# A third couple by seven products of sums in every gate and up group of a decoder trunk

## The chip, the cores and the metric

The kernel runs on one core of a Trainium2 chip. The metric is the device time of one execution in microseconds (us), the median of several runs. TensorE multiplies matrices (PE in the profile, its weight loads PEld), VectorE (DVE) and ScalarE (ACT) do elementwise work, GpSimd (POOL) and SyncE (SP) mostly issue DMA transfers here.

## The reference, cut to what matters

The program is a two-layer decoder trunk on 256 tokens of width 2048: a Conformer convolution, a SwiGLU feed-forward block, shared keys and values, a dilated attention, a second SwiGLU block and a last RMSNorm, all in float32. The part that is touched is the first half of each SwiGLU block:

```
def _swiglu(h, w_gate, w_up, w_down):
    return (jax.nn.silu(h @ w_gate) * (h @ w_up)) @ w_down
```

`h` is 256 x 2048, `w_gate` and `w_up` are 2048 x 5632 and `w_down` is 5632 x 2048. There are two such blocks.

## The kernel before, in words

**Three passes.** A float32 product is made of three passes in a rounded type (fp32r): every operand is split into a high part and a remainder, and TensorE adds x_hi·w_hi, x_hi·w_lo and x_lo·w_hi into one bank (`nat`, L404 to L406). The split of a block of weights (`split`) is one cast on ACT (L216, it makes `whi`) and one subtraction on DVE (L218, it makes `wlo`). `whi` and `wlo` have four buffers each, and blocks are split two ahead of the block that TensorE works on (`AHEAD`).

**Groups and couples.** `ffn_hidden` makes the hidden layer in 11 groups of 512 gate columns and the same 512 up columns. A group sums over 2048 = 16 tiles of 128, taken as eight couples of two tiles. A couple done plainly ("n" in `ITEMS_FF`) is two blocks of 128 x 1024 weights, gate and up, and 2 (gate, up) x 2 (tiles) x 2 (token halves) x 3 passes = 24 matmuls of 512 columns. A couple marked "S" is done by Winograd's form of Strassen's scheme: the two tiles, the two token halves, gate and up make a 2 x 2 product of blocks, which takes seven products in place of eight, so 21 matmuls, some of them with sums of the activations (`xsums`) and some with sums of the weights. The items of a group are `"nnnnSnSn"` in every group but the first, which is all "n".

**The weights of an S couple.** `emit_sums` splits an S couple in four blocks q = 0 to 3. Block 0 is a split of a whole 128 x 1024 block, followed on DVE by four differences of 128 x 512 (L234: t1, t2, t4 and one more, written into the small buffers `sq` and `sqacc`). Blocks 1 to 3 are five splits of 128 x 512 each: one of raw weights, four of these differences. The raw weights of an S couple have one place only (`places`, three parts of the tile `work`). They are fetched by three DMAs on POOL's queue (`load_sums`, L205 for 512 KB, L207 twice for 256 KB), and the fetch for the next S couple can start only when the differences and splits of this one have read their part. The plain blocks come over SP's queue (L279) into three buffers `raw`.

**The end of a group.** After the last S couple `combine` brings the four sum banks to `work` (one ACT copy L875, four DVE additions L877). `hidden` adds them to the other four banks, applies SiLU on ACT (L884) and multiplies on DVE (L883, L886, L887). `turned`, five ticks into the next group, transposes the result on TensorE (L895), and ACT and DVE split it into `hid` (L897, L898). A tick is a step of the program's own queue (`later`), one for each block that TensorE has used. The sum banks of one group are the plain banks of the group before, so the first S couple has to come after `turned`.

**The activations' sums.** `sum_up` makes the four sums of a couple's activations once for each layer, during the first, all-plain group: one addition (L753), four small operations (L757), a cast on ACT (L758) and a remainder on DVE (L759).

Of the kernel before, what the change touches and what calls it, by code (L numbers as in the profile page):

```python
# [9 lines left out]
F32 = mybir.dt.float32  # L10
# [6 lines left out]
P = 128  # L17
# [23 lines left out]
SUMS = 7  # L41
# [2 lines left out]
ITEMS_1 = HALF_0, "nnn" + "SnnSnSn" * 2 + "Sn" + "nnn"  # L44


SUMS_FF = 2
ITEMS_FF = "nnnnSnSn"


_VEC = {}
# [39 lines left out]
def trunk(ctx: ExitStack, tc: tile.TileContext, xT, vec, const, w1, w2, wk, wv, wq, wo, wg0, wu0, wd0, wg1, wu1, wd1, fing, out):  # L91
# [211 lines left out]
    def later(n, fn):  # L303
        queue.append([n, fn])
# [441 lines left out]
    def wide(a):  # L746
        return a.rearrange("p (a b) -> p a b", b=P)

    def sum_up(sums, u, two, h, d):

        h, d = h.rearrange("p (a b) -> p a b", b=S), wide(d)
        two = two.bitcast(F32)
        nc.vector.tensor_tensor(out=h, in0=two[:, :, 0, :], in1=two[:, :, 1, :], op=ALU.add)  # L753
        a11, a21, a12, a22 = (h[:, j, t * P:(t + 1) * P] for j in range(2) for t in range(2))
        for i, a, b, op in ((0, a21, a22, ALU.add), (1, d[:, 0, :], a11, ALU.subtract), (2, a11, a21, ALU.subtract),
                            (3, a12, d[:, 1, :], ALU.subtract)):
            nc.vector.tensor_tensor(out=d[:, i, :], in0=a, in1=b, op=op)  # L757
        nc.scalar.copy(sums[:, u, :, 0, :], d)  # L758
        nc.vector.tensor_tensor(out=sums[:, u, :, 1, :], in0=d, in1=sums[:, u, :, 0, :].bitcast(F32), op=ALU.subtract)  # L759

    n_used = [0]

    def two_blocks(a, b, items, n_sums, n_rest, act, sums, cs, sum_banks, combine):


        u_sums, u_plain = pairs_of(items, n_sums)
        ab = a, b
        begun = [False, False]
        ps = None

        def plain(i, k, stop, ts=(0, 1), parts=None):
            hi, lo = parts or next_block(*ab[i], k)[1:]
            for j in range(GKV):
                for t in ts:
                    nat(cs[t][i], tokens(act, k * GKV + j, t), hi[:, j, :], lo[:, j, :], not begun[i] and j == 0, stop and j == GKV - 1)
            begun[i] = True

        def seven(k, start):
            n = n_used[0]
            n_used[0] += 1  # L780
            assert all_sums[n][0][0] is a[0] and all_sums[n][2] == k
            two = [[sums[:, k, i, j, :] for j in range(2)] for i in range(4)]
# [12 lines left out]
        for i in range(2):  # L795
            for k in ahead:
                plain(i, k, False)
                tick()
        body = items[2:len(items) - n_rest]
        for n, item in enumerate(body):  # L800
            if item == "S":
                if ps is None:
                    ps = [p for t in sum_banks() for p in t]
                    seven(next(u_sums), True)
                else:
                    seven(next(u_sums), False)
# [44 lines left out]
    def ffn_hidden(ff, scratch, wg, wu, x, norm):  # L851

        nonlocal hT
        hid = new_x(ff, "hid", FT)
        sums = ff.tile([P, SUMS_FF, 4, 2, P], F32R, name="xsums", tag="t8")
        later(2, lambda: norm.rstd_nat(bank2))
        for k in range(SUMS_FF):
            later(3 + 3 * k, lambda k=k: sum_up(sums, k, x[:, 2 * k:2 * k + 2, :, :], room("sq"), room("sq")))
        for n in range(2 * D // NBV):
            later(3 + n, lambda c=n // 2, t=n % 2: turn_over(c, t, bank2()[:, 0, :, :].rearrange("p a b -> p (a b)")))  # L860
            if n % 2:
# [60 lines left out]
    with tc.tile_pool(name="ff", bufs=1) as ff:  # L922
        scratch = kept.tile([P, DT * S], F32, name="residual")
        hid = ffn_hidden(ff, scratch, wg0, wu0, x, norm)
        buf = ff.tile([P, 4, NBV], F32, name="t", tag="t8")
        sums = rp.tile([P, SUMS, 4, 2, P], F32R, name="sums", tag="x")
        residual_back(8, scratch)
        later(6, lambda: load_first_sums(wd0, [buf[:, 0:2, :], buf[:, 2, :], buf[:, 3, :]]))
        for u in range(SUMS):
            later(2 + 3 * u, lambda u=u: sum_up(sums, u, hid[:, 2 * u:2 * u + 2, :, :], room("sq"), room("sq")))  # L930
# [12 lines left out]

        for half, items in enumerate(ITEMS_0):
            cs = (first_banks if half else second_banks)()
            rest, plain = two_blocks((wd0, 2 * half), (wd0, 2 * half + 1), items, items.count("S"), 3, hid, sums, cs,
                                     second_banks if half else first_banks, lambda ps: combine(half, ps))
            if half:
                x = new_x(rp, "x")
                norm = Norm()  # L950
                for c in range(2):
                    later(c, lambda c=c: normed(c))
            for i in range(2):
                for u in rest:
# [75 lines left out]
    with tc.tile_pool(name="ff", bufs=1) as ff:  # L1030
# [1 line left out]
        hid = ffn_hidden(ff, scratch, wg1, wu1, x, norm)  # L1032

        ss = [little("ss", 8) for t in range(2)]
        buf = ff.tile([P, 4, NBV], F32, name="t", tag="t8")
        gain = [buf[:, 2 + i, :] for i in range(2)]

        sums = rp.tile([P, SUMS, 4, 2, P], F32R, name="sums", tag="x")
        residual_back(8, scratch)
        later(6, lambda: table(AF.Sqrt, silu[-1]))  # L1040
        later(6, lambda: load_first_sums(wd1, [cst.rearrange("p (k n) -> p k n", k=GKV), buf[:, 0, :], buf[:, 1, :]]))
        for u in range(SUMS):
            later(2 + 3 * u, lambda u=u: sum_up(sums, u, hid[:, 2 * u:2 * u + 2, :, :], *gain))

        def load_gain(half):
            for i in range(2):
# [105 lines left out]
```

## Time and profile before

| | us |
|---|---|
| median of 3 runs (lowest, highest) | 2147.03 (2146.43, 2154.44) |
| profiled execution | 2150.78 |
| its span, first to last instruction | 2148.3 |
| busy in it: PE / DVE / ACT / POOL | 2124.0 / 1659.1 / 1157.6 / 342.4 |
| the 11 gate and up groups of the first layer | about 345 to 776 |
| the 11 of the second layer | about 1447 to 1878 |

Matmuls are pipelined: one of 512 columns is listed with 0.39 us, but the next starts 0.23 us after it. Likewise DVE and ACT start their next instruction a little before the listed end of the one before. Times on a row of the timeline count from the start of the span.

### The profile page before, as it was taken

To read this page: it belongs to the slowest core of one execution; us is meant where nothing else is said; L and a number is where in the kernel's file an instruction comes from. 1 tells how busy PE (TensorE), PEld (TensorE's weight loads), DVE (VectorE), ACT (ScalarE), POOL (GpSimd) and SP (SyncE) were. 2 spreads that over 40 slices of the span, in tenths; PEclk is the share of its full clock that TensorE was granted. 3 is DMA by queue.
4 is the path that set the end of the run, shared out by engine and by line. 5 is a ranking of instruction groups with operands and counts; after the bars stand their busy time and mean duration, and the time that the engine had idled before them with its cause. 6 is when DMAs were issued, how large, how long until landed. Compare 5 with 4: busy or idle time off the path is not lost.

```text
span 2148.3 us, 28961 instructions
## 1 busy us (share of the span) xinstructions
PE 2124.0 (99%) x10550; PEld 1801.0 (84%) x10550; DVE 1659.1 (77%) x2403; ACT 1157.6 (54%) x1611; POOL 342.4 (16%) x357
## 2 busy tenths in 40 slices
PE   8999899999999999999999999999999999999998
PEld 8999788888888887888888888888888888887886
DVE  6888875788888888878745677665887888788877
ACT  6665545455555555455644566554555555555454
POOL 4999111000000001001000100010000000011210
PEclk9999999999999999999999999999999999999999
DMA  7555367656665556655665644566666566666654
GB/s 244 183 159 168 97 182 233 194 196 193 199 198 194 189 193 225 206 187 184 194 197 184 190 150 148 174 198 213 199 188 214 179 198 200 200 205 222 211 203 155
DMA packets 115966, 410.66 MB, mean 191 GB/s; under 512 B 13936, under 2 KB 14960, under 8 KB 115824
## 3 DMA queue, kind: packets, MB, share of 16 engines
q1 hardware_dynamic: 93024, 331.19, 47.9%
q0 software_dynamic: 22080, 76.56, 10.9%
q8 instruction: 82, 1.34, 0.2%
q10 hardware_dynamic: 720, 1.07, 0.1%
q14 instruction: 60, 0.49, 0.1%
HBM read 402.47 MB, written 6.29 MB: 190 GB/s over the span
## 4 chain that ended last, share of the span: by engine, by line
PE 90%; DVE 4%; DMA 3%; ACT 1%; issue 1%; SPq 0%; POOL 0%; DVEq 0%; ACTq 0%; POOLq 0%
PE pp L405 10%; PE pp L406 10%; PE pp L404 10%; PE pp L331 10%; PE aux L404 8%; PE aux L406 8%; PE aux L405 8%; PE pp L373 7%; PE pp L335 5%; PE b L406 2%; PE b L404 2%; PE b L405 2%; DMA raw<-wd 2%; DVE wlo L218 2%; DVE aux L571 1%
## 5 line engine op out<-in xcount | busy, mean ns | idle before, releaser
L218 DVE TENSOR_TENSOR wlo<-raw,whi 128x1024 fp32r<-128x1024 f32 x400 | 483.3, 1231 | 189.6 <-ACT whi L216 188.2
L216 ACT CAST whi<-raw 128x1024 fp32r<-128x1024 f32 x400 | 412.7, 1051 | 351.9 <-DMA raw<-wu 93.0
L285 ACT CAST whi<-raw 128x1024 fp32r<-128x1024 f32 (+1 forms) x209 | 216.1, 1037 | 226.1 <-PE pp L331 84.2
L287 DVE TENSOR_TENSOR wlo<-raw,whi 128x1024 fp32r<-128x1024 f32 (+1 forms) x164 | 202.1, 1243 | 140.0 <-ACT whi L285 120.8
L404 PE MATMUL pp<-whi,x 128*128 128x512 f32 x668 | 261.2, 391 | 0.0
L406 PE MATMUL pp<-whi,x 128*128 128x512 f32 x668 | 260.1, 389 | 0.0
L405 PE MATMUL pp<-wlo,x 128*128 128x512 f32 x668 | 259.9, 389 | 0.0
L216 ACT CAST whi<-sq 128x512 fp32r<-128x512 f32 x128 | 79.6, 622 | 231.2 <-issue 83.1
L404 PE MATMUL aux<-whi,x 128*128 128x512 f32 x516 | 203.4, 394 | 0.0
L406 PE MATMUL aux<-whi,x 128*128 128x512 f32 x516 | 201.1, 390 | 0.0
L405 PE MATMUL aux<-wlo,x 128*128 128x512 f32 x516 | 200.9, 389 | 0.0
L406 PEld LDWEIGHTS pp<-whi,x 128*128 128x128 f32 x668 | 125.4, 188 | 26.1
L405 PEld LDWEIGHTS pp<-wlo,x 128*128 128x128 f32 x668 | 125.4, 188 | 25.7
L404 PEld LDWEIGHTS pp<-whi,x 128*128 128x128 f32 x668 | 125.4, 188 | 25.6
L571 DVE SCALAR_TENSOR_TENSOR aux<-up,vecs,aux 128x256 f32<-128x256 f32 x350 | 140.9, 481 | 1.6 <-ACT aux L569 1.6
L205 POOL DMA_DIRECT2D work<-wg x40 | 21.8, 546 | 747.4 <-DVE sqacc L234 565.5
L373 PE MATMUL pp<-x,whi 128*128 128x256 f32 x720 | 133.5, 287 | 0.0
L218 DVE TENSOR_TENSOR wlo<-sq,whi 128x512 fp32r<-128x512 f32 x128 | 88.3, 690 | 57.5 <-ACT whi L216 57.3
L331 PE MATMUL pp<-x,whi 128*128 128x512 f32 x512 | 122.7, 393 | 0.0
L405 PE MATMUL pp<-wlo,hid 128*128 128x512 f32 x306 | 119.8, 392 | 1.4 <-DVE wlo L218 1.1
L406 PE MATMUL pp<-whi,hid 128*128 128x512 f32 x306 | 119.2, 389 | 0.0
L404 PE MATMUL pp<-whi,hid 128*128 128x512 f32 x306 | 119.1, 390 | 0.0
(285 smaller groups left out, 4494.1 us busy)
## 6 DMA issues: line engine op xcount, KB each, us to landing
raw<-wg SPq DMA_DIRECT2D x136, 512.0 KB, 4.1
raw<-wu SPq DMA_DIRECT2D x136, 512.0 KB, 4.2
raw<-wd SPq DMA_DIRECT2D x128, 512.0 KB, 4.4
raw<-w SPq DMA_DIRECT2D x75, 512.0 KB, 3.9
work<-wg POOLq DMA_DIRECT2D x40, 512.0 KB, 3.8
work<-wu POOLq DMA_DIRECT2D x80, 256.0 KB, 4.2
raw<-wv SPq DMA_DIRECT2D x32, 512.0 KB, 4.3
raw<-wk SPq DMA_DIRECT2D x32, 512.0 KB, 4.2
```

The lines of the kernel that those rows point to most:

```text
L205: nc.gpsimd.dma_start(places[0], src[0])
L216: made.append(nc.scalar.copy(hi, raw))
L218: made.append(nc.vector.tensor_tensor(out=lo, in0=raw, in1=hi.bitcast(F32), op=ALU.subtract))
L285: nc.scalar.copy(hi[:, part, :], raw[:, part, :])
L287: eng.tensor_tensor(out=lo[:, part, :], in0=raw[:, part, :], in1=hi[:, part, :].bitcast(F32), op=ALU.subtract)
L331: nc.tensor.matmul(bk[:, m, :, :], hi, x[:, k, :, :], start=k == 0, stop=k == kt_n - 1 and turned, skip_group_check=True)
L335: nc.tensor.matmul(bk[:, m, 0, :], lo, x[:, k, 0, :], start=False, stop=k == kt_n - 1 and not turned, skip_group_check=True)
L373: nc.tensor.matmul(bks[u][:, m, :], a[:, j, m * P:(m + 1) * P], b, start=kt == 0 and m == 0 and i == 0, stop=kt == DT - 1 and i == len(pas ...
L404: nc.tensor.matmul(o, xs[0], hi, start=start, stop=False, skip_group_check=True)
L405: nc.tensor.matmul(o, xs[0], lo, start=False, stop=False, skip_group_check=True)
L406: nc.tensor.matmul(o, xs[1], hi, start=False, stop=stop, skip_group_check=True)
L571: nc.vector.scalar_tensor_tensor(out=acc[i % 2], in0=win, scalar=w, in1=acc[i % 2], op0=ALU.mult, op1=ALU.add)
```

## The change

Three couples of each group after the first are done by seven products, not two: the items are now `"nnnSnSSn"`, so the second and the third S couple follow each other with nothing between them. The sums of a third couple's activations need room. Three of the four sums of each couple stay in `xsums`; the fourth goes into the place of the couple's own first tile, second token half, in `x`, which an S couple does not read. So `sum_up` can write it only after the first group has used that couple, and its ticks move from 3 + 3k to 7 + 3k. It now casts and takes the remainder in two pieces (three sums, one sum). The tile `buf` of the later stages is made as large as the new `xsums`, with which it shares its room.

```diff
-SUMS_FF = 2
-ITEMS_FF = "nnnnSnSn"
+SUMS_FF = 3
+ITEMS_FF = "nnnSnSSn"
...
-        nc.scalar.copy(sums[:, u, :, 0, :], d)
-        nc.vector.tensor_tensor(out=sums[:, u, :, 1, :], in0=d, in1=sums[:, u, :, 0, :].bitcast(F32), op=ALU.subtract)
+        i = 0
+        for o in places:
+            di = d[:, i:i + o.shape[1], :]
+            nc.scalar.copy(o[:, :, 0, :], di)
+            nc.vector.tensor_tensor(out=o[:, :, 1, :], in0=di, in1=o[:, :, 0, :].bitcast(F32), op=ALU.subtract)
+            i += o.shape[1]
...
-        sums = ff.tile([P, SUMS_FF, 4, 2, P], F32R, name="xsums", tag="t8")
+        three = ff.tile([P, SUMS_FF, 3, 2, P], F32R, name="xsums", tag="t8")
+        sums = [(three[:, k, :, :, :], x[:, 2 * k:2 * k + 1, :, P:]) for k in range(SUMS_FF)]
...
-            later(3 + 3 * k, lambda k=k: sum_up(sums, k, x[:, 2 * k:2 * k + 2, :, :], room("sq"), room("sq")))
+            later(7 + 3 * k, lambda k=k: sum_up(sums[k], x[:, 2 * k:2 * k + 2, :, :], room("sq"), room("sq")))
```

What this does to the queues is seen at two places. The first is DVE's order at the end of the second S couple of a group (`wlo<-sq`, `wlo<-sqacc` are the splits of its last differences, `wlo<-raw` the split of a plain block). Before:

```order
L218 TENSOR_TENSOR wlo_4450<-sq_4413,whi_4449 128x512
L218 TENSOR_TENSOR wlo_4450<-sqacc_4415,whi_4449 128x512
L218 TENSOR_TENSOR wlo_4462<-sq_4419,whi_4461 128x512
L218 TENSOR_TENSOR wlo_4462<-sqacc_4417,whi_4461 128x512
L218 TENSOR_TENSOR wlo_4475<-raw_4473,whi_4474 128x1024
L218 TENSOR_TENSOR wlo_4487<-raw_4485,whi_4486 128x1024
```

and now:

```order
L218 TENSOR_TENSOR wlo_4457<-sqacc_4412,whi_4456 128x512
L218 TENSOR_TENSOR wlo_4469<-work_3786,whi_4468 128x1024
L234 TENSOR_TENSOR sq_4472<-work_3786 128x512
L234 TENSOR_TENSOR sqacc_4474<-work_3786,sq_4472 128x512
L234 TENSOR_TENSOR sqacc_4476<-work_3786,sqacc_4474 128x512
L234 TENSOR_TENSOR sq_4478<-work_3786 128x512
L218 TENSOR_TENSOR wlo_4487<-work_3786,whi_4486 128x512
L218 TENSOR_TENSOR wlo_4497<-sq_4472,whi_4496 128x512
L218 TENSOR_TENSOR wlo_4497<-sqacc_4474,whi_4496 128x512
L218 TENSOR_TENSOR wlo_4509<-sq_4478,whi_4508 128x512
L218 TENSOR_TENSOR wlo_4509<-sqacc_4476,whi_4508 128x512
L218 TENSOR_TENSOR wlo_4522<-raw_4520,whi_4521 128x1024
```

Where the plain blocks followed, the ten instructions of a third S couple now stand, and the plain blocks come after them. The second place is TensorE's order behind the first block of that last S couple. Before, its second block and the start of its third stood with their passes in turn:

```order
L404 MATMUL aux_4197<-whi_4433,xsums_3466 128x512
L405 MATMUL aux_4197<-wlo_4434,xsums_3466 128x512
L406 MATMUL aux_4197<-whi_4433,xsums_3466 128x512
L404 MATMUL pp_4360<-whi_4449,xsums_3466 128x512
L405 MATMUL pp_4360<-wlo_4450,xsums_3466 128x512
```

and now:

```order
L404 MATMUL aux_4228<-whi_4486,x_2831 128x512
L404 MATMUL pp_4355<-whi_4496,xsums_3466 128x512
L404 MATMUL pp_4354<-whi_4496,xsums_3466 128x512
L405 MATMUL aux_4228<-wlo_4487,x_2831 128x512
L406 MATMUL aux_4228<-whi_4486,x_2831 128x512
L404 MATMUL aux_4227<-whi_4508,x_2831 128x512
L405 MATMUL pp_4355<-wlo_4497,xsums_3466 128x512
L406 MATMUL pp_4355<-whi_4496,xsums_3466 128x512
L405 MATMUL pp_4354<-wlo_4497,xsums_3466 128x512
```

Passes that need only `whi` have moved ahead of those that need `wlo`; the L405 of the third block's second product (last row) has 14 matmuls of this couple ahead of it, six of the first block and the eight shown.

More of the change, by code (lines that the diff above doesn't have):

```diff
@@ L747, in wide, with sum_up @@
         return a.rearrange("p (a b) -> p a b", b=P)
-    def sum_up(sums, u, two, h, d):
+    def sum_up(places, two, h, d):
         h, d = h.rearrange("p (a b) -> p a b", b=S), wide(d)
@@ L781, in seven @@
             assert all_sums[n][0][0] is a[0] and all_sums[n][2] == k
-            two = [[sums[:, k, i, j, :] for j in range(2)] for i in range(4)]
+            two = [[p[:, i, j, :] for j in range(2)] for p in sums[k] for i in range(p.shape[1])]
             k0, k1 = 2 * k, 2 * k + 1
@@ L924, in trunk @@
         hid = ffn_hidden(ff, scratch, wg0, wu0, x, norm)
-        buf = ff.tile([P, 4, NBV], F32, name="t", tag="t8")
-        sums = rp.tile([P, SUMS, 4, 2, P], F32R, name="sums", tag="x")
+        buf = ff.tile([P, SUMS_FF * 3 * 2 * P], F32, name="t", tag="t8")[:, 0:4 * NBV].rearrange("p (a b) -> p a b", b=NBV)
+        four = rp.tile([P, SUMS, 4, 2, P], F32R, name="sums", tag="x")
+        sums = [(four[:, u, :, :, :],) for u in range(SUMS)]
         residual_back(8, scratch)
@@ L929, in trunk @@
         for u in range(SUMS):
-            later(2 + 3 * u, lambda u=u: sum_up(sums, u, hid[:, 2 * u:2 * u + 2, :, :], room("sq"), room("sq")))
+            later(2 + 3 * u, lambda u=u: sum_up(sums[u], hid[:, 2 * u:2 * u + 2, :, :], room("sq"), room("sq")))
         def turn_back(c, cs, n):
@@ L1034, in trunk @@
         ss = [little("ss", 8) for t in range(2)]
-        buf = ff.tile([P, 4, NBV], F32, name="t", tag="t8")
+        buf = ff.tile([P, SUMS_FF * 3 * 2 * P], F32, name="t", tag="t8")[:, 0:4 * NBV].rearrange("p (a b) -> p a b", b=NBV)
         gain = [buf[:, 2 + i, :] for i in range(2)]
-        sums = rp.tile([P, SUMS, 4, 2, P], F32R, name="sums", tag="x")
+        four = rp.tile([P, SUMS, 4, 2, P], F32R, name="sums", tag="x")
+        sums = [(four[:, u, :, :, :],) for u in range(SUMS)]
         residual_back(8, scratch)
@@ L1042, in trunk @@
         for u in range(SUMS):
-            later(2 + 3 * u, lambda u=u: sum_up(sums, u, hid[:, 2 * u:2 * u + 2, :, :], *gain))
+            later(2 + 3 * u, lambda u=u: sum_up(sums[u], hid[:, 2 * u:2 * u + 2, :, :], *gain))
         def load_gain(half):
```

## The prediction

> **What bounds the kernel now.** I read the page first, then the gate and up groups as windows, then who waits for whom there.
>
> ```profile
> PE 2124.0 (99%) x10550; PEld 1801.0 (84%) x10550; DVE 1659.1 (77%) x2403; ACT 1157.6 (54%) x1611; POOL 342.4 (16%) x357
> PE 90%; DVE 4%; DMA 3%; ACT 1%; issue 1%; SPq 0%; POOL 0%; DVEq 0%; ACTq 0%; POOLq 0%
> ```
>
> TensorE is busy all the time and is 90% of the chain of waits, so matmuls that go away are worth their time, if what feeds them keeps up. The windows are the first group of layer one, which is all plain, a later group, and the start of the down projection (us, then PE, PEld, DVE, ACT, POOL busy):
>
> ```profile
> 345.00:388.00 43.00, 43.00 (x201) 35.55 (x200) 19.29 (x17) 20.65 (x23) 3.24 (x6) 1.00 0.77 246
> 517.30:560.40 43.10, 43.10 (x195) 35.75 (x195) 35.27 (x45) 23.04 (x29) 3.27 (x6) 1.00 0.63 204
> 776.00:862.00 86.00, 84.61 (x376) 68.49 (x376) 74.93 (x118) 45.61 (x60) 8.67 (x16) 1.00 0.61 204
> ```
>
> The two S couples raised DVE from 19.3 to 35.3 of 43.1 us; TensorE does not wait. Who waits, from 431 to 776 us:
>
> ```profile
> DVE wlo L218 <- ACT whi L216: 59.1, 65, 2.6
> ACT whi L216 <- PE pp L406: 32.5, 22, 3.0
> PEld aux L405 <- DVE wlo L218: 0.2, 1, 0.2
> ```
>
> DVE waits for ACT, and ACT for TensorE to give a `whi` buffer back: the splits are ahead, held by four buffers. TensorE waited 0.2 us in eight groups. How far ahead they are decides this change.
>
> **What is removed.** The same eight transposes, two groups apart, and TensorE's rows of the second S couple (first, second, and the first behind it):
>
> ```profile
> 517.97 0.87 PE pp L895 x8
> 604.17 0.88 PE pp L895 x8
> ```
> ```profile
> 534.34 0.39 PE L404 MATMUL pp<-whi,x 128*128 128x512 f32 x1
> 534.56 0.39 PE L405 MATMUL pp<-wlo,x 128*128 128x512 f32 x1
> 539.10 0.39 PE L404 MATMUL aux<-whi,x 128*128 128x512 f32 x1
> ```
>
> A group lasts 86.20 / 2 = 43.1 us. From 534.34 to 539.10 are 21 matmuls, 0.227 us each. A couple by seven products saves 3 x 0.227 = 0.68 us, in 10 groups of 2 layers: 20 x 0.68 = 13.6 us, if nothing waits.
>
> **What is added on DVE.** DVE from the last split of the first S couple (525.64) over the plain couple and the second S couple to the plain block behind it:
>
> ```profile
> 525.64 0.69 DVE L218 TENSOR_TENSOR wlo<-sqacc,whi 128x512 fp32r<-128x512 f32 x1
> 526.83 2.36 DVE L218 TENSOR_TENSOR wlo<-raw,whi 128x1024 fp32r<-128x1024 f32 x2 [0.50 <-ACT whi L216]
> 529.10 1.22 DVE L218 TENSOR_TENSOR wlo<-work,whi 128x1024 fp32r<-128x1024 f32 x1
> 531.68 0.69 DVE L234 TENSOR_TENSOR sqacc<-work,sqacc 128x512 f32<-128x512 f32 x1
> 532.29 0.68 DVE L234 TENSOR_TENSOR sq<-work 128x512 f32<-128x512 f32 x1
> 532.89 0.69 DVE L218 TENSOR_TENSOR wlo<-work,whi 128x512 fp32r<-128x512 f32 x1
> 534.10 0.69 DVE L218 TENSOR_TENSOR wlo<-sqacc,whi 128x512 fp32r<-128x512 f32 x1
> 535.23 0.69 DVE L218 TENSOR_TENSOR wlo<-sq,whi 128x512 fp32r<-128x512 f32 x1 [0.45 <-ACT whi L216]
> 535.84 0.69 DVE L218 TENSOR_TENSOR wlo<-sqacc,whi 128x512 fp32r<-128x512 f32 x1
> 537.02 2.36 DVE L218 TENSOR_TENSOR wlo<-raw,whi 128x1024 fp32r<-128x1024 f32 x2 [0.50 <-ACT whi L216]
> ```
>
> From 529.10 to 536.53 less the 0.45 of waiting are 7.0 us of DVE work, against 2.4 for a plain couple (537.02). So a group gets 4.6 us more: 39.9 of 42.4. On average it still fits. But the S couple takes DVE 7.0 us and TensorE only 4.76, so DVE loses 2.2 us of its lead in each, and now two stand together. Here I follow the queue through one group, in the times of these rows. Up to the second S couple nothing moves against TensorE. What is new is that `turned` now falls just ahead of the first S couple: its 0.87 us of transposes let that couple's last cast come 0.87 us earlier against TensorE, its two subtractions take DVE 2 x 0.60, so the last split ends at 526.33 - 0.87 + 1.20 = 526.66, before 526.83, where the plain blocks start anyway. Then:
>
> ```profile
> 532.92 0.55 POOL L205 DMA_DIRECT2D work<-wg  x1 [9.78 <-ACT whi L216]
> DMA to landing us min/median/max: 3.9/3.9/3.9
> DMA to landing us min/median/max: 3.6/3.6/3.6
> 535.94 2.00 ACT L216 CAST whi<-raw 128x1024 fp32r<-128x1024 f32 x2 [0.22 <-ACT whi L216]
> ```
>
> 1. The one place for an S couple's raw weights is free when the third difference ends, 531.68 + 0.69 = 532.37; POOL issues the next 512 KB at 532.92, and it lands 3.9 us later (this load; 3.6 is the quickest of eight groups' second loads, that of the group from 690), at 536.82. Before, nobody missed it for 20 us. Now the third S couple's cast waits for it, and behind that cast on ACT and DVE stand all later splits.
> 2. From a cast's start to DVE's start are 1.08 us (535.94 to 537.02). DVE's whole split starts at 537.90, not at 537.02, where the buffer alone would let it.
> 3. From there DVE runs at the pace of the second couple: the third block's second split starts 5.00 us later (529.10 to 534.10), at 542.90, and ends at 543.59.
> 4. TensorE reaches the third couple at 539.10; 14 matmuls later, at 542.28, stands the L405 that needs this split.
>
> What a late split costs TensorE is in the trace, in the down projection:
>
> ```profile
> 854.77 0.68 DVE L218 TENSOR_TENSOR wlo<-t,whi 128x512 fp32r<-128x512 f32 x1
> 855.50 0.50 PE L405 MATMUL pp<-wlo,sums 128*128 128x512 f32 x1 [0.68 <-DVE wlo L218]
> 855.84 0.39 PE L406 MATMUL pp<-whi,sums 128*128 128x512 f32 x1
> ```
>
> 0.05 us from DVE's end to the matmul, and the next comes 0.34 instead of 0.23 later: 0.16 us. So TensorE is late by 543.59 + 0.16 - 542.28 = 1.47 us. The splits behind it come 0.60 us apart (two matmuls or more stand between their users), and the plain block's split at 545.9 finds TensorE at the same lateness; I count 1.47 once. A group gains 0.68 and loses 1.47: +0.79 us, times 20 = **+15.8 us**.
>
> By the Trainium skill ("DMA: Bandwidth & Descriptors", "Anatomy of one DMA — SWDGE (gpsimd) path") such a transfer takes 2.0 us and its bytes at 436 GB/s, an estimate of 3.2 us for 512 KB; the trace disagrees with 3.6 to 3.9. With 3.2 the loss would be 0.77 us a group and the time about 2149.
>
> Bounds: with 3.6 for the load the loss is 1.17, +9.8 us. With 3.9 and a refill of 0.11 us at each of five more late L405 it is 2.0, +27.
>
> **The rest.** Does DVE catch up before the next group? Its work from the last plain split on:
>
> ```profile
> 539.30 0.69 DVE L877 TENSOR_TENSOR work<-pp,work 128x512 f32<-128x512 f32 x1
> 547.02 1.22 DVE L218 TENSOR_TENSOR wlo<-raw,whi 128x1024 fp32r<-128x1024 f32 x1
> ```
>
> The third plain block of the next group comes 7.7 us after `combine` begins. With `combine` at 544.70 + 2.3 = 547.0, it is split at 554.7 to 555.9; the next group starts at 539.10 + 45 x 0.227 + 1.47 = 550.8, and TensorE needs that block 24 x 0.227 = 5.4 us later, at 556.2. It fits by 0.3 us. The third `sum_up` and the two-piece remainders fall into the first group, where DVE has 23.7 us free; I take nothing (a sum_up is some 2.5 us by the four 0.285 us and two 0.69 us operations of such rows):
>
> ```profile
> L757 DVE TENSOR_TENSOR sq<-sq 128x128 f32<-128x128 f32 x44 | 11.2, 285 | 0.3
> ```
>
> Without that cover it would cost 2 x 2.5 = 5 us. At the start of the down projection TensorE already loses 86.00 - 84.61 = 1.4 us, and DVE comes there later by the debt: between 0 and twice 1.4 us; I take 0, since it opens with six plain couples.
>
> **Sum.** The profiled execution took 2150.78, 2.5 more than its span of 2148.3 and 3.7 above the median; its span should become 2164. On the median, 2147.0 + 15.8 = 2162.8, so **2163 us**.
>
> **Rivals.** *TensorE alone decides* (faster): DVE keeps ahead through both S couples, and the 13.6 us come in full: 2133. For it: DVE and ACT have 8 and 20 us free in a group, and no matmul waits now. Against it: the lead is 4 blocks at most. It needs the third couple's whole split by 537.90 - 1.47 = 536.4, before its buffer even comes free. The Trainium skill ("Perfetto Trace Analysis", "Identifying the Most-Contended Engine") has one relieve the engine with the highest occupancy first, for TensorE by LDWEIGHTS; by its rows that is TensorE by a hair (35.75 against DVE's 35.27), so the rule leans to this rival.
> *The load is no limit* (no change): the raw weights are there in time, and only the buffer holds the split back, at 537.02: 0.88 us better, the loss is 0.59, 20 x (0.59 - 0.68) = -2, so 2145. For it: such loads took 3.6 at times; against: none of the landings is near 3.0.
> *The debt is carried over* (slower still): the 0.3 us of margin above are not there, say because SiLU's result comes late, and each group loses about 0.7 us more: +14, 2177.
>
> **How the numbers follow.** My forecast 0.57 (its own range 2153 to 2174, by the bounds), load no limit 0.21, TensorE alone 0.13, debt carried 0.09. 0.5% is 10.7 us, about what a measurement here can tell from no change: below 2136.3 is faster, above 2157.8 slower. Faster: 0.13. Same: 0.21 and 0.09 of the forecast. Slower: 0.48 and 0.09, 0.57. The range reaches from 2142 to 2176; TensorE alone and the outer end of the debt are left out.
>
> **What would show it.** In the profile after: 60 matmuls fewer, a group of about 43.9 us; waits of "PE L405 <- DVE wlo" of some 1.5 us a group in the last S couple, none in the first two; the third couple's ACT cast released by the DMA into `work`; DVE near 40 us a group. Wrong would be a group of 42.4 us without such waits (TensorE alone), waits with the cast released by TensorE (load no limit), or waits on plain blocks at the start of a group (debt).

## The result, and the profile after

The changed kernel takes 2178.3 us (median; 2176.4 to 2178.5), beside it the kernel before 2148.1 us: 1.014 times as long (95% interval 1.0128 to 1.0152). Slower was the forecast, but by 15.8 us; it is 30.2. The profiled execution took 2178.25 us.

The same two lines of the page, now of the changed kernel:

```profile
PE 2133.8 (98%) x10490; PEld 1783.4 (82%) x10490; DVE 1742.7 (80%) x2581; ACT 1193.3 (55%) x1699; POOL 373.9 (17%) x417
PE 71%; DVE 12%; DMA 7%; issue 5%; ACT 3%; POOL 1%; SPq 0%; DVEq 0%; POOLq 0%; ACTq 0%
```

60 matmuls have gone, yet PE is listed busy for longer: part of the waits for weights is listed as busy (87.09 us in the two groups of the next row, whose own work is 2 x 42.42 = 84.84, as worked out below). TensorE's share of the chain of waits fell from 90% to 71%; DVE, the DMAs and "issue" took most of what it lost. Two groups as a window (us, then PE, PEld, DVE, ACT, POOL busy), between two rows of the transposes in the chain of waits (start, length):

```profile
566.30:655.41 89.11, 87.09 (x384) 69.63 (x383) 78.60 (x104) 49.23 (x67) 9.73 (x18) 1.00 0.57 190
```
```profile
477.40 0.44 PE b L901 x4
566.30 0.44 PE b L901 x4
...
744.35 0.44 PE b L901 x4
```

The rows are two groups apart. From 477.40 to 744.35 are six groups, 44.49 us each; before it was 43.10. 20 x 1.39 = 28 us, the difference of the spans (2176.5 - 2148.3 = 28.2). So the loss is in the gate and up groups. (The medians differ by 2 us more: the execution of the kernel before that was profiled took 2150.78 us, 2.7 above its median of 2148.1.) TensorE's own work in a group is 43.10 - 0.68 = 42.42, so each of them loses 2.07 us, where 1.47 was forecast. DVE's 39.3 us a group are the 39.9 of the forecast.

The groups reach further than the table ahead of the prediction says: in the kernel before, the first layer's start with the matmul at 323.9 us and end at 803.0, where the first matmul on `hid` starts, not from about 345 to 776.

Who waits for whom, from 431 to 776 us, nearly eight groups (us in all, times, longest):

```profile
PE pp L405 <- DVE wlo L218: 3.5, 6, 0.8
PE aux L405 <- DVE wlo L218: 3.1, 4, 0.8
PE pp L404 <- DVE hid L904: 0.3, 1, 0.3
```
```profile
PEld aux L404 <- ACT whi L216: 4.5, 12, 0.5
PEld pp L404 <- DVE hid L904: 2.2, 4, 0.8
PEld pp L404 <- ACT whi L216: 1.8, 4, 0.5
```

The waits for `wlo` were foreseen. Not foreseen: waits for `whi`, so for ACT, and waits for `hid`, the result of the last group. The latter come four times, in every second group.

**The groups are of two kinds.** The sum banks of a group are in turn `aux` and `b` (`first_banks`) and two tiles `pp` of two banks each (`second_banks`). A group whose transposes went to `aux` and `b`, by the timeline of DVE, POOL, ACT and TensorE; the second S couple starts on TensorE at 576.82, the third at 581.58:

```profile
571.56 1.22 DVE L218 TENSOR_TENSOR wlo<-work,whi 128x1024 fp32r<-128x1024 f32 x1
575.37 0.54 POOL L205 DMA_DIRECT2D work<-wg  x1 [9.71 <-ACT whi L216]
576.82 0.39 PE L404 MATMUL aux<-whi,x 128*128 128x512 f32 x1
579.35 1.05 ACT L216 CAST whi<-work 128x1024 fp32r<-128x1024 f32 x1 [1.15 <-DMA work<-wg]
580.44 1.23 DVE L218 TENSOR_TENSOR wlo<-work,whi 128x1024 fp32r<-128x1024 f32 x1 [1.43 <-ACT whi L216]
581.58 0.39 PE L404 MATMUL aux<-whi,x 128*128 128x512 f32 x1
584.24 0.68 DVE L218 TENSOR_TENSOR wlo<-work,whi 128x512 fp32r<-128x512 f32 x1
584.97 0.50 PE L405 MATMUL pp<-wlo,x 128*128 128x512 f32 x1 [0.77 <-DVE wlo L218]
587.38 0.50 PE L405 MATMUL pp<-wlo,x 128*128 128x512 f32 x1
588.45 0.50 PE L404 MATMUL aux<-whi,x 128*128 128x512 f32 x1
```

Here the forecast can be laid over the rows. The second S couple's split leads TensorE by 576.82 - 571.56 = 5.26 us; before it was 534.34 - 529.10 = 5.24. The load is issued at 575.37 and the cast starts 3.98 later, released by the DMA; DVE idles 1.43 us before the third couple's split. The matmul at 584.97 has nine matmuls of its couple ahead of it and would have started at 581.58 + 9 x 0.227 = 583.62: 1.35 late, and 0.11 more for the refill, 1.46. The forecast was 1.47, but for another matmul: it took the L405 of the third block, which has 14 matmuls ahead of it, and the one that waited is of the second block, whose split comes earlier and whose matmul has nine ahead. In the prediction's rows that split starts 3.79 us after the couple's first (532.89 - 529.10), so the same walk has it end at 537.90 + 3.79 + 0.69 = 542.38 and TensorE late by 542.38 + 0.16 - (539.10 + 9 x 0.227) = 1.40: right to 0.06 us, and the agreement to a hundredth is luck. Then more comes: at 587.38 and at 588.45 (the first block of the plain couple that ends the group; its L404 stands ahead there, and its cast is late) two refills, and between them matmuls 0.23 to 0.24 us apart in place of 0.227.

A group whose transposes went to `pp`:

```profile
520.88 1.03 PE L901 MATMUL pp<-cst,work 128*128 128x128 f32 x8
522.38 1.28 DVE L904 TENSOR_TENSOR hid<-pp,hid 128x512 fp32r<-128x512 f32 x2
523.12 0.19 PEld L404 LDWEIGHTS pp<-whi,x 128*128 128x128 f32 x1 [0.48 <-DVE hid L904]
527.53 1.22 DVE L218 TENSOR_TENSOR wlo<-work,whi 128x1024 fp32r<-128x1024 f32 x1
532.34 0.39 PE L404 MATMUL pp<-whi,x 128*128 128x512 f32 x1
566.14 0.60 PE L901 MATMUL b<-cst,work 128*128 128x128 f32 x4
609.92 1.03 PE L901 MATMUL pp<-cst,work 128*128 128x128 f32 x8
```

The first S couple wants a tile `pp` that DVE's `hid` subtraction is still reading, so TensorE stands still, and the weight buffer of this block comes back late. (The row at 522.38 holds two subtractions; the first, which reads the tile that is wanted, ends at 523.06, and the matmul starts at 523.12.) The second S couple's split leads by 532.34 - 527.53 = 4.81 us only, 0.45 less than in the other kind. The four transposes to `aux` stand 0.44 us ahead of those to `b`, so this group lasts from 520.88 to 565.70, 44.8 us, and the next, of the other kind, to 609.92, 44.2 us.

### The profile page after: what moved, and what is told of

It is laid out like the page before. It is cut to its first block, busy times and chain, and to the rows that moved or that the text cites. A ratio compares the mean times of both kernels' runs of the same rounds, so it can differ in the third digit from the quotient of the medians.

```text
span 2176.5 us, 29187 instructions
## 1 busy us (share of the span) xinstructions
PE 2133.8 (98%) x10490; PEld 1783.4 (82%) x10490; DVE 1742.7 (80%) x2581; ACT 1193.3 (55%) x1699; POOL 373.9 (17%) x417
## 4 chain that ended last, share of the span: by engine, by line
PE 71%; DVE 12%; DMA 7%; issue 5%; ACT 3%; POOL 1%; SPq 0%; DVEq 0%; POOLq 0%; ACTq 0%
PE pp L331 10%; PE pp L405 8%; PE pp L406 7%; PE pp L404 7%; PE pp L373 7%; PE aux L405 6%; PE aux L406 6%; PE aux L404 6%; PE pp L335 5%; DVE wlo L218 5%; DMA work<-wu 4%; DVE sqacc L234 3%; ACT whi L216 3%; DMA raw<-wd 2%; PE b L406 2%
## 5 line engine op out<-in xcount | busy, mean ns | idle before, releaser
L218 DVE TENSOR_TENSOR wlo<-raw,whi 128x1024 fp32r<-128x1024 f32 x360 | 434.0, 1228 | 137.0 <-ACT whi L216 135.5
L216 ACT CAST whi<-raw 128x1024 fp32r<-128x1024 f32 x360 | 370.4, 1050 | 311.4 <-DMA raw<-wd 76.4
L405 PE MATMUL pp<-wlo,x 128*128 128x512 f32 x648 | 256.2, 395 | 9.0 <-DVE wlo L218 8.6
L404 PE MATMUL pp<-whi,x 128*128 128x512 f32 x648 | 252.6, 392 | 1.0 <-DVE hid L904 0.3
L406 PE MATMUL pp<-whi,x 128*128 128x512 f32 x648 | 252.7, 390 | 0.0
L216 ACT CAST whi<-sq 128x512 fp32r<-128x512 f32 x168 | 104.4, 621 | 257.2 <-PE pp L406 87.5
L405 PE MATMUL aux<-wlo,x 128*128 128x512 f32 x516 | 202.5, 392 | 8.3 <-DVE wlo L218 8.3
L404 PE MATMUL aux<-whi,x 128*128 128x512 f32 x516 | 205.0, 400 | 0.0
L205 POOL DMA_DIRECT2D work<-wg x60 | 32.6, 544 | 784.4 <-ACT whi L216 546.3
L405 PEld LDWEIGHTS pp<-wlo,x 128*128 128x128 f32 x648 | 121.7, 188 | 43.0 <-DVE wlo L218 19.0
L218 DVE TENSOR_TENSOR wlo<-sq,whi 128x512 fp32r<-128x512 f32 x168 | 115.4, 687 | 39.9 <-ACT whi L216 39.6
L404 PEld LDWEIGHTS pp<-whi,x 128*128 128x128 f32 x648 | 121.6, 188 | 30.7 <-DVE hid L904 5.1
L218 DVE TENSOR_TENSOR wlo<-work,whi 128x1024 fp32r<-128x1024 f32 x120 | 114.2, 952 | 34.5 <-ACT whi L216 34.5
L406 PEld LDWEIGHTS pp<-whi,x 128*128 128x128 f32 x648 | 121.7, 188 | 24.2
L216 ACT CAST whi<-work 128x1024 fp32r<-128x1024 f32 x120 | 100.1, 837 | 56.8 <-DMA work<-wg 26.3
L405 PEld LDWEIGHTS aux<-wlo,x 128*128 128x128 f32 x516 | 97.0, 188 | 31.5 <-DVE wlo L218 12.9
```

Source lines behind the costliest of these rows:

```text
L216: made.append(nc.scalar.copy(hi, raw))
L218: made.append(nc.vector.tensor_tensor(out=lo, in0=raw, in1=hi.bitcast(F32), op=ALU.subtract))
L404: nc.tensor.matmul(o, xs[0], hi, start=start, stop=False, skip_group_check=True)
L405: nc.tensor.matmul(o, xs[0], lo, start=False, stop=False, skip_group_check=True)
L406: nc.tensor.matmul(o, xs[1], hi, start=False, stop=stop, skip_group_check=True)
```

## The experiments

My theory after this reading: three terms, which are the pace of DVE over two S couples that stand together, the refetch of the raw weights, and the tile that the transposes hold. The main rival: DVE's total load of 39 to 40 us a group, or ACT's, cannot be served without waits. "Group" below is the mean of six groups from the same transposes in the chain of waits, as above (in spread_late, whose chain does not show them, in the timeline); for the kernel before it is the prediction's 43.10 from two groups, and 43.08 from six.

| kernel | group, us | time, us | kernel before beside it, us | ratio (95%) |
|---|---|---|---|---|
| before | 43.10 | | 2146.5 to 2148.1 | |
| the change | 44.49 | 2178.3 | 2148.1 | 1.014 (1.0128 to 1.0152) |
| pair_late | 43.96 | 2166.8 | 2148.1 | 1.0088 (1.0074 to 1.0102) |
| one_early | 43.26 | 2150.6 | 2148.1 | 1.0013 (1.0004 to 1.0022) |
| two_places | 43.40 | 2153.8 | 2148.1 | 1.0028 (1.0017 to 1.0039) |
| turn_early | 44.15 | 2174.7 | 2148.1 | 1.0124 (1.0111 to 1.0138) |
| turn_not_last | 44.2 | 2174.5 | 2147.6 | 1.0123 (1.0106 to 1.014) |
| two_turn | 43.22 | 2155.0 | 2147.4 | 1.0034 (1.0021 to 1.0048) |
| spread | 43.70 | 2161.1 | 2147.4 | 1.0062 (1.005 to 1.0075) |
| pool_two | 45.55 | 2212.6 | 2147.4 | 1.0302 (1.0288 to 1.0316) |
| spread_two | 42.83 | 2141.2 | 2146.5 | 0.9972 (0.9961 to 0.9983) |
| spread_late | 43.9 | 2174.5 | 2146.5 | 1.0137 (1.0118 to 1.0155) |
| spread_late_two | 42.89 | 2151.8 | 2146.5 | 1.0022 (1.0013 to 1.003) |
| spread_two_turn | 42.43 | 2133.4 | 2146.7 | 0.9936 (0.9922 to 0.995) |

### Two S couples together, without a third: pair_late

```diff
 (kernel before)
-ITEMS_FF = "nnnnSnSn"
+ITEMS_FF = "nnnnnSSn"
```

> The kernel before with its two S couples moved together to the end of the group (nnnnnSSn in place of nnnnSnSn), nothing else; the work of TensorE and of DVE per group is that of before (35.3 us of DVE). Theory: the loss comes from two S couples standing together, since the second finds its raw weights' only place refilled too late and DVE's lead used up. Then each of the 20 groups loses 1.5 us (the prediction's walk) to 2.1 us (what a group of the change lost), and the time is 2178 to 2190, with waits of PE L405 on wlo in the second S couple. Rival: DVE's total load of a group, 40 of 42 us, is what TensorE waits for; then this kernel stays at 2148, since the load has not changed.

Measured: 2166.8 us, 18.7 more, with DVE's work that of before. So two S couples together cost something by themselves, without any higher load: 43.96 - 43.10 = 0.86 us a group. It is less than the theory said, and the timeline shows why:

```profile
527.41 0.55 POOL L205 DMA_DIRECT2D work<-wg  x1 [32.73 <-DVE sqacc L234]
532.06 1.57 ACT L216 CAST whi<-work 128x1024 fp32r<-128x1024 f32 x2 [0.22 <-PE aux L406]
```

The cast of the second S couple is released by TensorE, which gives a buffer back, and not by the DMA. Behind five plain couples the first S couple of the pair is split earlier against TensorE (523.58 to 530.46, 6.9 us ahead, in place of 5.3), so its place is refilled in time. What is left is the first term alone, DVE's pace: 0.86, where the prediction's rival without the refetch had worked out 0.59.

### The first S couple right behind the transposes: one_early

```diff
 (kernel before)
-ITEMS_FF = "nnnnSnSn"
+ITEMS_FF = "nnnSnnSn"
```

> The kernel before with its first S couple one couple earlier (nnnSnnSn), right behind the transposes, nothing else. Theory: in the groups whose four sums lie in the banks that the hid subtraction of the transposed tile still reads, the first product waits about 0.33 us, 10 groups: +3 us, 2151, and no wait on wlo anywhere, since a plain couple or two follow each S couple. Rival: the early S couple itself costs DVE its lead, then waits on wlo show up behind it and the time is over 2158.

Measured: 2150.6 us, 2.6 more, as expected. The wait is the one of the change, in the timeline of one_early (the same in every second group):

```profile
516.29 1.04 PE L895 MATMUL pp<-cst,work 128*128 128x128 f32 x8
518.53 0.19 PEld L404 LDWEIGHTS pp<-whi,x 128*128 128x128 f32 x1 [0.49 <-DVE hid L898]
```

A group costs 0.16 us more on average. By itself the tile is a small term.

### A second place for the raw weights: two_places

```diff
 (the change; place(n) takes the two places in turn, the second is the room of the last four hid tiles;
  the class Parted, which puts the two parts of hid together, and place itself are left out)
-        hid = new_x(ff, "hid", FT)
+        hid = Parted(new_x(ff, "hid", FT - 4), lambda: ff.tile([P, 4, 2, S], F32R, name="tail", tag="tail"))
...
-            if n + 1 < len(all_sums) and all_sums[n + 1][0][0] is all_sums[n][0][0]:
-                load_sums(n + 1)
+            nxt = n + len(places)
+            if nxt < len(all_sums) and all_sums[nxt][0][0] is all_sums[n][0][0]:
+                load_sums(nxt)
...
-                load_first_sums(wg, here)
+                tail = ff.tile([P, 4, NBV], F32, name="spare", tag="tail")
+                load_first_sums(wg, here, (tail[:, 0:2, :], tail[:, 2, :], tail[:, 3, :]))
```

> The changed kernel with a second place for the raw weights of an S couple, in the part of the hidden layer (its last four tiles) that is written only after the last group; each S couple's fetch is issued one S couple earlier. Theory: the fetch that comes 0.9 us too late in the second of the two S couples that stand together is part of the loss; without it DVE's split starts when the buffer is free, and each group wins 0.9 us or, where it spares several waits, more: 2150 to 2160, the third couple's ACT cast no longer released by a DMA. Rival: DVE's pace over the two S couples (7.0 us for each, where TensorE takes 4.76) or its total load decides alone, and an earlier fetch changes nothing: 2176 to 2180.

Measured: 2153.8 us, 24.5 less than the change. The chain of waits (L925 are the transposes there) and a third S couple's cast (L239):

```profile
474.01 0.44 PE b L925 x4
...
734.41 0.44 PE b L925 x4
```
```profile
572.94 1.57 ACT L239 CAST whi<-work 128x1024 fp32r<-128x1024 f32 x2 [0.22 <-ACT whi L239]
```

260.40 / 6 = 43.40 us a group: the refetch cost 44.49 - 43.40 = 1.09 us, where the walk had 0.88 (537.90 - 537.02). The cast is no longer released by a DMA. What is left, 43.40 - 42.42 = 0.98, is about the 0.86 of pair_late and the tile.

### The transposes one block earlier: turn_early, turn_not_last, two_turn

```diff
 (turn_early: the change; two_turn: two_places)
-            later(5, lambda c=c, cs=cs: turned(c, cs))
+            later(4, lambda c=c, cs=cs: turned(c, cs))
 (turn_not_last: the change)
-            later(5, lambda c=c, cs=cs: turned(c, cs))
+            later(4 if c < F // NBV - 1 else 5, lambda c=c, cs=cs: turned(c, cs))
```

> The changed kernel with the transposes of the previous group's result one block earlier (four blocks into the group in place of five). Theory: half of the groups lose more than the others because the first S couple's product waits for the hid subtraction in its bank (0.33 us) and hands its weight buffer back later (0.44 us less lead); with the subtraction done one block, 2.7 us, sooner, these groups come to the loss of the others: -4 to -8 us, 2170 to 2174, and no wait of PEld on hid. Rival: the transposes then find SiLU's result not yet there and TensorE waits for it: 2178 or more, with waits of PE on work or on DVE at L901.

> The kernel two_places (2153.8 us) with the transposes one block earlier, as in turn_early. Theory: every second group there takes 43.64 us where the others take 43.17; the difference is the first S couple's product waiting for the hid subtraction in its bank, so 10 x 0.4 = 4 us go and no PEld waits for hid: 2150. Rival: as with the changed kernel, where the earlier transposes gave 3.7 us in sum although the groups of the first layer became 0.35 us shorter each (20 x 0.35 = 7), something at the end of a layer takes half of it back: 2152.

> The changed kernel with the transposes one block earlier in all groups but the last of each layer, whose transposes fall into the down projection and stay where they were. With all of them earlier (turn_early) the groups of the first layer became 0.35 us shorter, 7 us for 20 groups, but the time only 3.7. Theory: the other half was lost where the last group's transposes stand between the first blocks of the down projection; with these left alone the full 7 us come: 2171 to 2172. Rival: what was lost lies in the second layer's groups or after them, whatever the last transposes do: 2174 to 2175 again.

In turn_early no weight load waits for `hid` any more, and a group of the first layer takes 44.15 in place of 44.49 us. That is 0.34, so 7 us for 20 groups, but the time fell by 3.7 only. In two_turn a group became 0.18 us shorter and the time did not (2155.0 against 2153.8). I put the missing half down to the last transposes, which stand in the down projection. turn_not_last leaves these alone, and its time is the same as turn_early's: that theory fell. The traces point at the down projections all the same. From the first matmul on `hid` to the last of the projection the two take together 473.2 us in turn_early and 473.5 in turn_not_last, where the change takes 470.9, and 475.1 in two_turn, where two_places takes 471.4. But these are single executions, and pair_late, which does not move the transposes, takes 473.3; what waits there was not followed, so the cause stays open.

### The S couples apart, by single blocks: spread

```diff
 (the change; "a" is the gate block of a plain couple, "b" its up block; the code that reads them is left out)
-ITEMS_FF = "nnnSnSSn"
+ITEMS_FF = "nnnSaSbSn"
```

> The changed kernel with its blocks in another order and nothing else: the gate block of the fourth plain couple stands between the first and the second S couple, its up block between the second and the third, the fifth plain couple behind the third (nnn S a S b S n). Each S couple now has at least one plain block behind it, 2.7 us of TensorE with 1.2 us of DVE. Theory (two S couples together are what costs): the refetch gets 2.7 us more than it needs (it was about 0.9 to 1.1 late) and DVE makes up 1.5 us behind each S couple; at most 0.4 us of loss a group is left, in half of the groups the bank that the hid subtraction reads: 2134 to 2143. Rival (DVE's total load, 40 of 42 us, or ACT's): the same instructions in the same 20 groups, so 2175 or more.

Measured: 2161.1 us. The order alone wins 17 us, with the same instructions, so the total load cannot be the whole loss. But I had it at 2134 to 2143. The timeline says what I missed (L222 is the cast, L224 the split):

```profile
530.31 1.05 ACT L222 CAST whi<-work 128x1024 fp32r<-128x1024 f32 x1 [1.79 <-DMA work<-wg]
531.39 1.23 DVE L224 TENSOR_TENSOR wlo<-work,whi 128x1024 fp32r<-128x1024 f32 x1 [0.93 <-ACT whi L222]
```

The refetch is still late, for DVE idles 0.93 us. I had counted the time that TensorE gains between two S couples (2.7 us), but the place comes free when DVE has used it, and DVE needs only its 1.2 us for the block between. The refetch is measured against DVE's clock, not TensorE's.

### The S couples apart and a second place: spread_two

The change with the diffs of spread and of two_places together:

```diff
-ITEMS_FF = "nnnSnSSn"
+ITEMS_FF = "nnnSaSbSn"
...
-                load_first_sums(wg, here)
+                load_first_sums(wg, here, (tail[:, 0:2, :], tail[:, 2, :], tail[:, 3, :]))
```

> The kernel spread (nnn S a S b S n, 2161.1 us) with the second place for the raw weights of two_places. In spread the groups take 43.24 and 44.1 us in turn, 0.87 and 1.75 above the 42.37 of the matmuls alone, and DVE still idles 0.93 us in the middle of a group for the refetched weights of the third S couple. Theory: that idle time is the 0.87 us; with a second place the groups take 42.4 and 43.2 us, on average 0.3 less than the 43.08 of before: 2141 to 2144. Rival: DVE's pace (8.2 us for an S couple and a block, where TensorE takes 7.48) sets the end without the refetch too: 2150 to 2161.

Measured: 2141.2 us, as expected; the first kernel with three S couples that is faster than the kernel before. Its groups are still of two kinds (L931 are the transposes):

```profile
515.59 1.03 PE L931 MATMUL pp<-cst,work 128*128 128x128 f32 x8
558.79 0.60 PE L931 MATMUL aux<-cst,work 128*128 128x128 f32 x4
559.23 0.60 PE L931 MATMUL b<-cst,work 128*128 128x128 f32 x4
601.23 1.03 PE L931 MATMUL pp<-cst,work 128*128 128x128 f32 x8
```

The group with the tile's wait takes 43.20, the other 42.44, the full speed of TensorE. Here the tile costs 0.76 us, not the 0.3 that the wait itself lasts.

### Two of the differences by GpSimd: pool_two

```diff
 (two_places)
-            t4 = difference(b21, t2, "sqacc")
-            first_raw.extend((t1, t2, t4, difference(b22, b12, "sq")))
+            t4 = difference(b21, t2, "sqacc", nc.gpsimd)
+            first_raw.extend((t1, t2, t4, difference(b22, b12, "sq", nc.gpsimd)))
```

> The kernel two_places (a second place for the raw weights, 2153.8 us) with the last two of the four weight differences of each S couple made by GpSimd in place of VectorE. Theory (what is left there, 0.8 us in each group, is DVE's pace over two S couples that stand together): DVE has 5.8 us of work in an S couple in place of 7.0, over two of them 2.4 us less, and the 0.8 us go in full, 20 x 0.8 = 16: 2138; left are the 0.4 us in half of the groups. Rivals: GpSimd's differences are late (they took 1.0 to 1.7 us each for this size elsewhere) and the last block of the couple waits for them: 2150 to 2160, with ACT casts released by POOL; or GpSimd slows DVE down, whose 128x512 operations then take over 0.75 us.

Measured: 2212.6 us, 59 more than two_places. Both rivals show. GpSimd slows DVE, in the timeline (L257 are the differences, L241 the splits):

```profile
532.28 1.61 POOL L257 TENSOR_TENSOR sqacc<-work,sqacc 128x512 f32<-128x512 f32 x1 [7.79 <-issue]
532.66 1.77 DVE L241 TENSOR_TENSOR wlo<-sq,whi 128x512 fp32r<-128x512 f32 x1
533.86 1.73 POOL L257 TENSOR_TENSOR sq<-work 128x512 f32<-128x512 f32 x1
534.37 1.77 DVE L241 TENSOR_TENSOR wlo<-sqacc,whi 128x512 fp32r<-128x512 f32 x1
```

A split of 0.69 us takes 1.77 beside such a difference, and two of them do. Taking 1.2 us from DVE in an S couple gave it 2.2 us of waiting. And GpSimd's differences are late themselves, so that casts of ACT (L239) wait for them, first from 431 to 776 us (us in all, times, longest), then in the couple above:

```profile
ACT whi L239 <- POOL sq L257: 44.4, 19, 2.8
```
```profile
535.62 0.62 ACT L239 CAST whi<-sq 128x512 fp32r<-128x512 f32 x1 [2.56 <-POOL sq L257]
```

What each of the two costs was not separated. A group takes 45.55 us, which makes 43 of the 59 us; the S couples of the down projections use the same differences, and the two projections take 485.8 us in place of 471.4, 14 of the other 16. The Trainium skill ("SBUF — State Buffer", "SBUF: two separate sides") says that VectorE and GpSimd take the same pair of ports by a lock that is held for a whole instruction; it includes a VectorE operation with two inputs from SBUF against a GpSimd operation that reads SBUF. The trace agrees: each of the two splits ends 0.55 us after the listed end of a difference (534.43 after 533.89, 536.14 after 535.59), as if its own 0.69 us had begun only when GpSimd was nearly done.

### One block ahead of the first S couple: spread_late, spread_late_two

```diff
 (spread, and spread_two)
-ITEMS_FF = "nnnSaSbSn"
+ITEMS_FF = "nnnaSbSaSb"
```

> The changed kernel with one place, its blocks in the order nnn a S b S a S b: each plain block behind the third couple stands between two S couples, and one stands between the transposes and the first S couple. Theory: the 0.9 us more that every second group of spread takes come from the bank that the hid subtraction still reads when the first S couple wants it, and from the weight buffer handed back late behind it; with a block of 2.7 us in front, that wait is gone and all groups take the 43.24 us of spread's others: 2150 to 2152. Rival: the groups differ for another reason (the third block of the next group, or SiLU late behind the last S couple, which now has only one block behind it): 2160 or more.

> The kernel spread_late with the second place for the raw weights. Theory: of the three terms (DVE's pace over two S couples that stand together, the refetch, the bank behind the transposes) none is left; a group takes the 42.37 us of its matmuls and transposes, or 0.1 more: 2133 to 2137, faster than before by 0.5 to 0.7%. Rival: DVE's load of 40 us in a group of 42.4 cannot be served without waits even so, and a group stays above 42.8: 2143 or more.

Both missed; the rivals had the times: 2174.5 and 2151.8 us. (The second rival's cause, DVE's load, does not hold, as the last experiment shows.) With two places a group takes 42.89 us, so less than before, and yet the time is 5 us longer. In the groups TensorE now waits for a cast (`PE pp L434 <- ACT whi L245`, up to 1.1 us), and most clearly at the start of the down projection. SP's queue there waits for DVE, which behind the last S couple still has to read the `raw` buffers (27.1 us in all, in the kernel before 18.9 at the same place); the casts wait for these loads, and one matmul waits 3 us:

```profile
SPq L309 <- DVE wlo L247: 27.1, 6, 9.2
```
```profile
803.85 1.04 ACT L245 CAST whi<-raw 128x1024 fp32r<-128x1024 f32 x1 [2.07 <-DMA raw<-wd]
806.50 0.66 PE L434 MATMUL pp<-whi,hid 128*128 128x512 f32 x1 [2.98 <-ACT whi L245]
```

So moving the first S couple away from the transposes at the cost of the block behind the last one is no way round the tile. The groups alone would make it 4 us faster than before (20 x 0.21); of the 9 us between that and the time, the traces show 7.5 in the two down projections, which take 240.6 and 238.9 us from the first matmul on `hid` to the last, in the kernel before 237.6 and 234.4. These 3 us are of the first; in the second TensorE waits several times for a split, 2.0 us the longest (at 1940.18).

### All three terms removed: spread_two_turn

```diff
 (spread_two)
-            later(5, lambda c=c, cs=cs: turned(c, cs))
+            later(4 if c < F // NBV - 1 else 5, lambda c=c, cs=cs: turned(c, cs))
```

> The kernel spread_two (2141.2 us; groups of 42.43 and 43.2 us in turn) with the transposes of each group's result but the last one block earlier. Theory: the 0.8 us of every second group are the bank behind the transposes, which the hid subtraction still reads when the first S couple wants it, and the weight buffer handed back late behind it; with the subtraction 2.7 us sooner these groups take 42.4 to 42.6 us: 10 times 0.6 to 0.8, 2133 to 2135. Rival: the gain in the groups is taken back at the start of the two down projections, as when the earlier transposes were tried with two places (groups 0.2 us shorter on average, the time not shorter): 2138 to 2142.

Measured: 2133.4 us, as expected: 13.3 us faster than the kernel before (ratio 0.9936, 0.9922 to 0.995). The page, the transposes in the chain of waits and a window of two groups:

```profile
PE 2109.1 (99%) x10490; PEld 1788.1 (84%) x10490; DVE 1739.9 (82%) x2581; ACT 1195.2 (56%) x1699; POOL 371.2 (17%) x417
```
```profile
467.98 0.43 PE b L931 x4
...
722.54 0.44 PE b L931 x4
```
```profile
552.84:637.68 84.84, 84.84 (x384) 70.20 (x383) 78.19 (x105) 49.36 (x67) 9.54 (x18) 1.00 0.60 199
```

254.56 / 6 = 42.43 us a group. TensorE is busy for 84.84 of 84.84 us, and DVE does the same 78 us of work in it as in the changed kernel. So the load of DVE was never too high for three S couples; what cost the time was the order of the work and two shared rooms.

## Why the prediction was right or wrong

**Right.** The sign, and the mechanism: TensorE saves 0.68 us a group if nothing waits (spread_two_turn has it: 43.10 - 42.43 = 0.67), and the third S couple's refetched weights and DVE's pace take more than that. 60 matmuls fewer, the third couple's cast released by the DMA into `work`, and DVE near 40 us a group came as said. In the groups that transpose to `aux` and `b` the walk gave the first wait well (1.47 and 1.46), partly by luck: it was worked out for a matmul one block later, and for the one that waited it gives 1.40. No catch-up debt reached the third plain block of the next group, as "It fits by 0.3 us" said; but the first block of the plain couple that ends the group itself was late by a refill. The sign "none in the first two" holds for the waits on `wlo`, which it names.

**Wrong: "Up to the second S couple nothing moves against TensorE."** The step followed the transposes' 0.87 us and the 1.20 us that their two subtractions take on DVE, and found the last split in time. It did not ask what the subtractions read. They read a tile `pp` that the first S couple wants at once, in every second group. That costs 0.3 us there and then, and the buffer handed back late takes 0.45 us off the lead at the second S couple, so that the third one's splits come later too. Groups of that kind take 44.8 us, 0.6 more than the others: 10 x 0.6 = 6 us.

**Wrong: "I count 1.47 once."** In the groups that transpose to `aux` and `b` 44.2 - 42.42 = 1.8 us are lost, 0.3 more than the first wait. After it the split queue stays just behind TensorE, and two more matmuls pay a refill, one of them for a cast of ACT that the walk had not queued at all. In all groups that is 20 x 0.3 = 6 us. The bound of +27 (2.0 us a group, by five refills of 0.11) was near the 2.07 lost; I should have forecast the refills, not bounded with them.

The two make 12 of the 12.4 us between the forecast of the span (2164) and its 2176.5; on the medians (2163 and 2178.3) the rest lies in the kernel before, whose median was 1.1 us higher beside the change and whose profiled execution was above its median. By causes, as the experiments split the 2.07 us: the refetch 1.09 (forecast 0.88), DVE's pace over the pair about 0.86 (0.59), the tile the rest, 0.1 (0), though by the two kinds of groups it is 0.3 on average. The terms are not independent: with the tile's wait gone from the change a group is 0.34 shorter, from spread_two 0.40.

**Readings.** Two windows of the prediction are not quite what it calls them: 345 to 388 us holds the end of the first group and, from 372.2, the first plain couples of the second, and 776 to 862 us holds the end of the last group up to 803.0; no term of the sum rests on that. The lower end of the range, 2153, is not the bound's 2147.0 + 9.8 = 2157.

**The rivals.** TensorE alone decides (2133) is what the kernel does once three rooms and orders are changed, and is wrong for the change as it stands. Load no limit is wrong for the change; with the load made no limit (two_places) the time is 2153.8, where I had put 2145, short by the same two terms. Debt carried was near in time (2177) for another reason: the extra loss is in the first and third S couple, not in the next group's third block.

**The Trainium skill's fetch time** ("DMA: Bandwidth & Descriptors", "Anatomy of one DMA — SWDGE (gpsimd) path"), by which an estimate of 3.2 us had been made, is again under the trace: the load above took 3.98 us from its issue to the cast that waited for it.

## What to carry to other kernels

Busy shares did not decide: DVE is as loaded in the kernel of 2133 us as in that of 2178. What decides is how far ahead the feeding engine is at each point, so walk its queue against the consumer, and for each room (a place in SBUF, a weight buffer, a PSUM tile) note on whose clock it comes free. When work is moved next to other work, ask what each of the two reads and hands back, not only how long it takes; and expect that after the first late block the following ones pay too.

## What the runs showed of the hardware

- A VectorE subtraction of 128x512 that takes 0.69 us takes 1.77 us beside a GpSimd subtraction of the same size (1.61 to 1.73 us) and ends 0.55 us after the listed end of that; giving GpSimd some of VectorE's work made the kernel 59 us slower (pool_two).
- A matmul that has waited for its weights costs more than its wait: in the changed kernel the one after the matmul at 584.97 starts 0.34 us later in place of 0.227, and the next four 0.231 us apart; behind the last refill (588.45) it is up to 0.236 for about nine.
- A PSUM tile of two banks was handed on as a whole here. The code shows that the first S couple's first product goes to the token half 0 of a tile `pp` and that the subtraction reads the other half, so the wait (0.3 us) is for a bank that the product does not use. Whether the chip asks for that or only the program's bookkeeping is not shown; a tile for each bank was not tried.
